# Seven-product FFN groups: two PSUM tiles in place of one, a list of weight jobs, and a last chunk of 512

## The chip, the cores and the metric

One Trainium2 chip, one of its cores. The metric is the device time of one launch in microseconds (us). The matrix engine is PE (its weight loads are PEld), the vector engine DVE, the scalar engine ACT; POOL and SP here issue transfers. SBUF is the on-chip memory, PSUM the accumulator of PE, in banks of 512 float32 per partition.

## The reference

A DiT block on 2048 tokens of width 1024: positions, modulated norm, a hybrid mixer (state-space branch and convolution branch), a second modulated norm, a SwiGLU FFN, and a final norm, in float32. The change touches the FFN of the second 1024 tokens and what follows it:

```
def _swiglu(h, wg, wu, wd):
    return (jax.nn.silu(h @ wg) * (h @ wu)) @ wd
...
x = x + g2 * _swiglu(_modulate(x, norm2_g[l], sh2, sc2), w_ffn_gate[l], w_ffn_up[l], w_ffn_down[l])
return _rmsnorm(x, norm_f_g)
```

The hidden width FFN_HIDDEN is 2816, that is 22 tiles of 128.

## The kernel before, in words

Every float32 product is made of three passes on PE: an operand is split into a rounded part hi (made by ACT) and a rest lo (made by DVE as a subtraction), and hi·hi, hi·lo and lo·hi are accumulated in PSUM. A matmul here is 128x128 weights by 512 tokens.

For the second half of the tokens the gate and up products of one hidden tile are a *group* of seven products in place of eight (a Strassen-like scheme over two halves of the tokens, L and R, and the weight matrices): products B11, T1, T2, B21, T3, B22, T4, named after their token operands, 12 matmuls each, 84 in all. They accumulate in three PSUM banks: b1 takes B11, then T2, T3 and T4 on top; b2 takes T1 and then B22; b3 takes B21. Between products the partial sums are read: ACT copies b1 after B11 (`fg`, left half), b2 after T1 (`fu`, right half), b1 after T2 (`fg`, right half); DVE adds b3 after B21, b1 after T3 (`fu`), b2 after B22 (`fg`); ACT applies silu; DVE multiplies `fu` by `fg` (right half, L1369) and, after T4, b1 by `fg` (left half, L1372); the result is split into ah and al. So the next product on b1 or b2 must come behind the read. In the kernel before, b1 and b2 are the two halves of one tile of two banks:

```
        ps, b3 = self.mm(), self.ms()
        b1, b2 = ps[:, 0:512], ps[:, 512:1024]
```

`mm()` gives one of three such tiles, `ms()` one of two tiles of one bank. The framework orders instructions by the tiles that they use, schedules them by priority, and puts in the semaphores.

Eleven chunks of two hidden tiles each follow one another. A chunk is two groups and a *down* part: 8 output tiles, each 12 matmuls with ah/al as moving operand and the weights `wd`; ACT scales the result out of PSUM (`fd`, L1424) and POOL adds it to the array d_x1 in device memory by an accumulating transfer (L1425). Chunk 0 computes its two tiles in the plain way, and its down part runs while DVE and ACT still make T1 to T4 in the background. The last chunk's down part adds into SBUF (L1440), first for the left 512 tokens (b=0), then for the right ones (b=1), with squares and their sum for the final norm; `final` then transposes, scales and stores the tokens.

The weights of a group (`group_weights`) are one load of 512 KB (wu, L1322) and two of 256 KB (gate, L1325 and L1326), four DVE sums (L1327 to L1331) in three buffers `ws`, and four conversions to hi (L1309) and lo (L1311) in two buffers each; the down weights are two loads with a conversion each (L1389, L1391). All are written at high priority and the scheduler places them. SP issues the loads in order; a load waits until its buffer's last reader is done. `t4()` is a ring of four buffers shared by fg, fu, fd and the background sums.

Of the kernel before, what the change touches and what calls it, by code (L numbers as in the profile page):

```python
# [22 lines left out]
HALF = 1024  # L23
# [20 lines left out]
class Kernel:  # L44
# [1243 lines left out]
    def prod(self, ps, w, c0, x, start=True, stop=True, group=True):  # L1288
# [4 lines left out]
        for k in range(n):  # L1293
            for j, (wt, mv) in enumerate(((whi, xhi), (whi, xlo), (wlo, xhi))):
                nc.tensor.matmul(  # L1295
                    ps,
                    wt[:, k, c0 : c0 + 128],
                    mv[k],
                    start=start and k == 0 and j == 0,
                    stop=stop and k == n - 1 and j == 2,  # L1300
                    skip_group_check=not group,
                )
            self.tick()

    def parts(self, f, c=1024):

        nc = self.nc
        hi = self.wp.tile([128, c // 128, 128], F32R, tag="hi", name=self.nm("hi"))
        nc.scalar.activation(hi, f, AF.Copy)  # L1309
        lo = self.wp.tile([128, c // 128, 128], F32R, tag="lo", name=self.nm("lo"))  # L1310
        nc.vector.tensor_tensor(lo, f, hi.bitcast(F32), op=OP.subtract)  # L1311
        return hi, lo

    def group_weights(self, vp, t):
# [5 lines left out]
        with self.tc.high_priority():  # L1320
            w4 = self.wp.tile([128, 8, 128], F32, tag="raw", name=self.nm("wu"))
            nc.sync.dma_start(w4, up)  # L1322
            w1, w2, w3 = (vp.tile([128, HALF], F32, tag="acc", name=self.nm("ws"), bufs=3).rearrange("p (k c) -> p k c", c=128) for _ in range(3))
            a, b = slice(0, 4), slice(4, 8)
            nc.sync.dma_start(w1[:, a], gate[:, a])  # L1325
            nc.sync.dma_start(w2[:, b], gate[:, b])  # L1326
            TT(w1[:, b], w4[:, a], w4[:, b], op=OP.add)  # L1327
            TT(w2[:, a], w1[:, b], w1[:, a], op=OP.subtract)
            p1 = self.parts(w1)
            TT(w3[:, a], w1[:, a], w4[:, a], op=OP.subtract)  # L1330
            TT(w3[:, b], w2[:, b], w2[:, a], op=OP.subtract)  # L1331
            p2 = self.parts(w2)
            p3 = self.parts(w3)
            p4 = self.parts(w4[:, b], 512)
        cut = lambda p, s: tuple(t[:, s] for t in p)
# [451 lines left out]
```

## Time and profile before

| | us |
|---|---|
| median of 3 runs | 3075.66 (3075.57, 3075.66, 3083.16) |
| the profiled execution | 3084.87, its span 3083.1 |
| PE busy | 2945.7 (96%) |
| DVE busy | 2089.6 (68%) |
| ACT busy | 1075.6 (35%) |

The profiled execution lies 9.21 us above the median of the runs; the 1.77 us between its time and its span lie outside the records. PE counts as busy from the start of a matmul to its modelled end, and matmuls overlap, so 96% still holds short stops. The second half's FFN lies from about 2345 us to the end of the span.

### The profile page before, as it was taken

How to read it: one execution, taken by the hardware profiler on the slowest of the kernel's cores; microseconds unless marked ns; L12 is line 12 of the kernel's file. 1: busy time of each engine (PE TensorE's matmuls, PEld its weight loads, DVE VectorE, ACT ScalarE, POOL GpSimd, SP SyncE). 2: the span in 40 equal slices, each digit the busy share in tenths (PEclk: the TensorE clock that was granted, in tenths of full speed). 3: DMA queues.
4: the chain of work that ended last, by engine and by line, in shares of the span. 5: the costliest groups of instructions: out<-in, count | busy, mean ns of one | idle time of the engine just before them, and what ended most of it. 6: DMA issues, size and time to landing. Idle time of an engine off the chain costs nothing.

```text
span 3083.1 us, 34510 instructions
## 1 busy us (share of the span) xinstructions
PE 2945.7 (96%) x12987; PEld 2357.3 (76%) x12987; DVE 2089.6 (68%) x3116; ACT 1075.6 (35%) x1463; POOL 245.3 (8%) x401
## 2 busy tenths in 40 slices
PE   7999999999999989999999999999998999999998
PEld 3778787878878768878888888888787677777776
DVE  6389899997887675668778787757567343333336
ACT  4223344333442662232212112233245333333333
POOL 0112321100011000000000000000000000011100
PEclk9999999999999999999999999999999999999999
DMA  5344545633443558764122212224566444445543
GB/s 199 123 122 129 152 161 172 184 97 115 125 119 116 185 191 293 259 204 151 62 62 76 62 62 62 89 97 148 177 207 144 102 103 103 103 107 118 121 106 130
DMA packets 391367, 411.29 MB, mean 133 GB/s; under 512 B 33377, under 2 KB 322497, under 8 KB 391200
## 3 DMA queue, kind: packets, MB, share of 16 engines
q1 hardware_dynamic: 339104, 275.73, 28.9%
q0 software_dynamic: 38640, 128.61, 15.4%
q10 hardware_dynamic: 13456, 4.75, 0.6%
q8 instruction: 102, 1.67, 0.2%
q14 instruction: 65, 0.53, 0.1%
HBM read 279.37 MB, written 129.61 MB: 133 GB/s over the span
## 4 chain that ended last, share of the span: by engine, by line
issue 51%; PE 32%; DVE 7%; DMA 5%; POOL 2%; ACT 2%; ACTq 0%; POOLq 0%; DVEq 0%; SPq 0%
PE mm L182 16%; PE mm L1295 11%; DVE acc L920 2%; DMA wm<-in_w_mod_dram 1%; PE ms L1295 1%; PE ms L741 1%; POOL d_x L1425 1%; DMA d_xt<-xts 1%; DVE lo L162 1%; DMA d_x<-fd 1%; PE ms L696 1%; POOL d_x L1112 1%; DMA Braw<-in_ssm_b_im_dram 0%; DMA dwr<-in_dw_kernel_dram 0%; PE mm L312 0%
## 5 line engine op out<-in xcount | busy, mean ns | idle before, releaser
L920 DVE SCALAR_TENSOR_TENSOR acc<-cin,dwk,acc 128x1009 f32<-128x1009 f32 (+1 forms) x464 | 570.6, 1272 | 1.1 <-ACT acc L916 0.5
L160 ACT ACTIVATE hi<-raw 128x1024 fp32r<-128x1024 f32 (+1 forms) x212 | 222.7, 1050 | 770.1 <-PE mm L182 726.5
L182 PE MATMUL mm<-hh,hi 128*128 128x512 f32 x1152 | 479.5, 416 | 0.5 <-ACT hh L446 0.5
L182 PE MATMUL mm<-hl,hi 128*128 128x512 f32 x1152 | 455.0, 395 | 0.0
L182 PE MATMUL mm<-hh,lo 128*128 128x512 f32 x1152 | 454.4, 394 | 0.0
L162 DVE TENSOR_TENSOR lo<-raw,hi 128x1024 fp32r<-128x1024 f32 (+1 forms) x212 | 256.5, 1210 | 93.4 <-ACT hi L160 93.0
L182 PE MATMUL mm<-h2h,hi 128*128 128x512 f32 x704 | 274.8, 391 | 0.0
L182 PE MATMUL mm<-h2l,hi 128*128 128x512 f32 x704 | 273.9, 389 | 0.1
L182 PE MATMUL mm<-h2h,lo 128*128 128x512 f32 x704 | 273.9, 389 | 0.0
L182 PEld LDWEIGHTS mm<-hh,lo 128*128 128x128 f32 x1152 | 218.2, 189 | 47.2 <-issue 0.4
L182 PEld LDWEIGHTS mm<-hh,hi 128*128 128x128 f32 x1152 | 218.4, 190 | 46.6 <-issue 2.2
L182 PEld LDWEIGHTS mm<-hl,hi 128*128 128x128 f32 x1152 | 218.7, 190 | 44.8 <-issue 1.6
L1311 DVE TENSOR_TENSOR lo<-ws,hi 128x1024 fp32r<-128x1024 f32 x60 | 73.5, 1225 | 230.6 <-ACT hi L1309 229.6
L182 PEld LDWEIGHTS mm<-h2l,hi 128*128 128x128 f32 x704 | 132.2, 188 | 27.9 <-DVE h2l L1145 0.5
L182 PEld LDWEIGHTS mm<-h2h,hi 128*128 128x128 f32 x704 | 132.2, 188 | 27.6 <-issue 0.3
L182 PEld LDWEIGHTS mm<-h2h,lo 128*128 128x128 f32 x704 | 132.2, 188 | 27.5
L1295 PE MATMUL mm<-al,hi 128*128 128x512 f32 x352 | 138.1, 392 | 4.9 <-DVE al L195 4.9
L1295 PE MATMUL mm<-ah,hi 128*128 128x512 f32 x352 | 135.0, 394 | 2.8 <-DVE fg L1406 2.4
L1295 PE MATMUL mm<-ah,lo 128*128 128x512 f32 x352 | 137.1, 389 | 0.0
L182 PE MATMUL mm<-ah,hi 128*128 128x512 f32 x352 | 136.7, 391 | 0.0
L182 PE MATMUL mm<-al,hi 128*128 128x512 f32 x352 | 136.7, 390 | 0.0
L182 PE MATMUL mm<-ah,lo 128*128 128x512 f32 x352 | 136.5, 389 | 0.0
(491 smaller groups left out, 5705.1 us busy)
## 6 DMA issues: line engine op xcount, KB each, us to landing
d_x<-fd POOLq DMA_DIRECT2D x80, 512.0 KB, 8.2
raw<-in_w_in_dram SPq DMA_DIRECT2D x72, 512.0 KB
wm<-in_w_mod_dram SPq DMA_DIRECT2D x48, 512.0 KB
d_g<-gsig POOLq DMA_DIRECT2D x32, 512.0 KB, 4.2
raw<-in_w_out_dram SPq DMA_DIRECT2D x32, 512.0 KB
raw<-in_w_ffn_gate_dram SPq DMA_DIRECT2D x28, 512.0 KB
raw<-in_w_ffn_up_dram SPq DMA_DIRECT2D x28, 512.0 KB
wd<-in_w_ffn_down_dram SPq DMA_DIRECT2D x24, 512.0 KB
```

The costliest lines, as they stand in the source:

```text
L160: nc.scalar.activation(hi, raw, AF.Copy)
L162: nc.vector.tensor_tensor(lo, raw, hi.bitcast(F32), op=OP.subtract)
L182: nc.tensor.matmul(ps[:, b * bw : (b + 1) * bw], wt[:, k, c0 : c0 + 128], mv[k][:, b * bw : (b + 1) * bw], start=(k == 0 and j == 0), stop ...
L696: nc.tensor.matmul(pz[:, d, :], BD[:, d, i, r, :], CR[d][r][:, i, d : d + 8].rearrange("p j c -> p (j c)"), start=(r == 0), stop=(r == 1))
L741: nc.tensor.matmul(ps.rearrange("p (i m) -> p m i", i=8), IN[:, d, i, :], rhs, start=True, stop=True)
L920: self.behind(nc.vector.scalar_tensor_tensor(t, x[:, i : i + W], K(i), t, op0=OP.mult, op1=OP.add), LAG)
L1112: nc.gpsimd.dma_start(self.d_x1[m, :, ts], xt)
L1295: nc.tensor.matmul(ps, wt[:, k, c0 : c0 + 128], mv[k], start=start and k == 0 and j == 0, stop=stop and k == n - 1 and j == 2, skip_group_ ...
L1311: nc.vector.tensor_tensor(lo, f, hi.bitcast(F32), op=OP.subtract)
L1425: nc.gpsimd.dma_start(self.d_x1[m4 * 4 + m, :, hs], o, accum_op=OP.add)
```

## The change

- b1 and b2 are tiles of their own, each the first half of a two-bank tile.
- The weights of groups and down parts are one list of *jobs* (four for a group, two for a down part). A job has a load, sums and a conversion. `next_job` is called at fixed places (after T1, B21, B22 and T4 are written, and after each half of a down part): it converts the job three ahead, sums the one five ahead and loads the one seven ahead. hi and lo have a third buffer. Conversions are ordered behind the last read of PSUM written before them. The down weights come through the same two buffers `raw` as the groups' up weights.
- The down part works on two output tiles at a time; in the first pair the hidden tile that was finished last comes at the end (`late`): its hi passes, then its lo pass.
- Nine chunks of two tiles, and the last four tiles (groups 18 to 21) as one chunk of 512 hidden units, whose down part is 192 matmuls into SBUF (96 for each half of the tokens). So 72 results go to d_x1 instead of 80; the number of matmuls is the same. `final` for the left half of the tokens starts, as it did, when the left half of the last down part is written; the right half behind it now has 96 matmuls instead of 48.

The core of the diff:

```diff
+    def stage(self, j, what):
+        nc = self.nc
+        if what == "load":
+            j["f"] = j["load"]()
+        elif what == "sums":
+            if j["sums"]:
+                j["sums"]()
+        else:
+            f = j["f"]() if callable(j["f"]) else j["f"]
+            n = self.ringed % 3
+            self.ringed += 1
+            out = []
+            for p in range(2):
+                if n < 2:
+                    t = self.wp.tile([128, 8, 128], F32R, tag=("hi", "lo")[p], name=self.nm("hl"[p]))
+                else:
+                    t = j["ring"][p]
+                c = 1
+                for x in j["shape"]:
+                    c *= x
+                out.append(t.rearrange("p k c -> p (k c)")[:, 0:c].rearrange("p (k c) -> p k c", k=j["shape"][0]))
+            hi, lo = out
+            i = nc.scalar.activation(hi, f, AF.Copy)
+            if self.last_act:
+                self.order(i, self.last_act)
+            i = nc.vector.tensor_tensor(lo, f, hi.bitcast(F32), op=OP.subtract)
+            if self.last_dve:
+                self.order(i, self.last_dve)
+            j["w"] = (hi, lo)
+
+    def jobs_start(self):
+        self.done = -1
+        self.last_act = self.last_dve = None
+        for n in range(7):
+            self.stage(self.jobs[n], "load")
+        for n in range(5):
+            self.stage(self.jobs[n], "sums")
+        for n in range(3):
+            self.stage(self.jobs[n], "conv")
+
+    def next_job(self):
+
+        self.done += 1
+        for what, n in (("conv", 3), ("sums", 5), ("load", 7)):
+            if self.done + n < len(self.jobs):
+                self.stage(self.jobs[self.done + n], what)
...
+        def sums1():
+            TT(w[1][:, b], w[4][:, a], w[4][:, b], op=OP.add)
+
+        def sums2():
+            TT(w[2][:, a], w[1][:, b], w[1][:, a], op=OP.subtract)
+
+        def sums3():
+            TT(w[3][:, a], w[1][:, a], w[4][:, a], op=OP.subtract)
+            TT(w[3][:, b], w[2][:, b], w[2][:, a], op=OP.subtract)
+
+        r = ring["w"]
+        return [
+            self.job((8, 128), r, load1, sums1),
+            self.job((8, 128), r, load2, sums2),
+            self.job((8, 128), r, load3, sums3),
+            self.job((4, 128), r, lambda: w[4][:, b]),
+        ]
...
-        ps, b3 = self.mm(), self.ms()
-        b1, b2 = ps[:, 0:512], ps[:, 512:1024]
+    def group(self, J, X, a):
+        b1, b2, b3 = self.mm()[:, 0:512], self.mm()[:, 0:512], self.ms()
...
+        self.prod(b1, W(2, 0), 0, X["T3"], start=False, group=False)
         with hp():
             add(u[:, R], b1)
+        self.prod(b2, W(2, 1), 0, X["B22"], start=False, group=False)
         with hp():
             add(g[:, R], b2)
+            act(g[:, R], g[:, R], AF.Silu)
             nc.vector.tensor_tensor(u[:, R], u[:, R], g[:, R], op=OP.mult)
+        self.next_job()
+        self.prod(b1, J[3]["w"], 0, X["T4"], start=False, group=False)
         with hp():
             nc.vector.tensor_tensor(u[:, L], b1, g[:, L], op=OP.mult)
+            act(a[0], u)
+            self.last_dve = nc.vector.tensor_tensor(a[1], u, a[0].bitcast(F32), op=OP.subtract)
+        self.next_job()
...
+    def down_prods(self, to, w, late):
+
+        for ps, x, c in to if not late else ():
+            self.prod(ps, w, c, x)
+        if late:
+            n = len(to[0][1][0]) - 1
+            first, last = slice(0, n), slice(n, n + 1)
+            for s, passes in ((first, (0, 1, 2)), (last, (0, 2)), (last, (1,))):
+                for ps, x, c in to:
+                    self.prod(ps, [t[:, s] for t in w], c, [p[s] for p in x], start=s is first, group=False, passes=passes)
...
+        acc = lambda dt: vp.tile([128, HALF], dt, tag="acc", name=self.nm("wx"), bufs=3)
+        ring = {"n": 0, "w": [acc(F32R).rearrange("p (k c) -> p k c", c=128) for _ in range(2)]}
+        ring["f"] = [acc(F32), vp.tile([128, HALF], F32, tag="csum", name="wx")]
+        ring["f"] += [vp.tile([128, HALF + 30], F32, tag="cin", name=self.nm("wx"), bufs=2)[:, 0:1024] for _ in range(2)]
+        self.jobs, self.ringed = [], 0
+        downs, groups = {}, {}
+        for c in range(9):
+            if c:
+                for t in (2 * c, 2 * c + 1):
+                    groups[t] = self.group_jobs(ring, t)
+            downs[c] = self.down_jobs(ring, 2 * c, 2)
+        for t in range(18, 22):
+            groups[t] = self.group_jobs(ring, t)
+        downs[9] = self.down_jobs(ring, 18, 4) + self.down_jobs(ring, 18, 4)
+        self.jobs_start()
+        for c in range(9):
             if c:
                 for t in range(2):
-                    self.group(vp, c * 2 + t, X, *a[t])
+                    self.group(groups[2 * c + t], X, a[t])
                     yield "up"
-            if c == 10:
-                break
-            for m4 in range(2):
-                w = down(c, m4)
-                for m in range(4):
-                    ps = self.mm()
-                    for b in range(2):
-                        self.prod(ps[:, b * 512 : (b + 1) * 512], w, m * 128, halves[b])
-                    o = self.t4(name="fd")
-                    nc.scalar.activation(o, ps, AF.Copy, scale=self.mod2[:, 24 + m4 * 4 + m : 25 + m4 * 4 + m])
-                    nc.gpsimd.dma_start(self.d_x1[m4 * 4 + m, :, hs], o, accum_op=OP.add)
-                    yield "down"
+            for i, J in enumerate(downs[c]):
+                for m in range(0, 4, 2):
+                    pp = [self.mm(), self.mm()]
+                    to = [(ps[:, b * 512 : (b + 1) * 512], half(b), (m + n) * 128) for n, ps in enumerate(pp) for b in range(2)]
+                    self.down_prods(to, J["w"], i == 0 and m == 0)
+                    for n, ps in enumerate(pp):
+                        o = self.t4(name="fd")
+                        r = i * 4 + m + n
+                        nc.scalar.activation(o, ps, AF.Copy, scale=self.mod2[:, 24 + r : 25 + r])
+                        nc.gpsimd.dma_start(self.d_x1[r, :, hs], o, accum_op=OP.add)
+                self.next_job()
+                yield "down"
+        for t in range(2):
+            self.group(groups[18 + t], X, a[t])
+            yield "up"
+        a = a + [(self.slot("P", name="ah"), self.slot("P", name="al")) for _ in range(2)]
+        for t in range(2):
+            self.group(groups[20 + t], X, a[2 + t])
+            yield "up"
...
+                J = downs[9][b * 4 + m // 2]
+                if m % 2 == 0:
+                    pp = [self.mm()[:, bs] for _ in range(2)]
+                    self.down_prods([(ps, half(b), n * 128) for n, ps in enumerate(pp)], J["w"], b == 0 and m == 0)
+                    self.next_job()
+                ps = pp[m % 2]
...
-        take(f1, 2 + 8)
+        take(f1, 2 + 2)
         self.finish(e)
-        take(f1, 10 * 2 + 9 * 8 + 8)
+        take(f1, 8 * 2 + 8 * 2 + 4 + 8)
         acc = end[0]
```

Three places show what stands where now. The first is PE in a group of a middle chunk, before; mm is the tile with b1 and b2, ms is b3, and the second name is the weight part:

```order
L1295 MATMUL mm_20718<-T2h_16967,lo_20708 128x512
L1295 MATMUL ms_20719<-B21h_16651,lo_20708 128x512
L1295 MATMUL mm_20718<-T3h_16970,hi_20710 128x512 [waits Activation_49]
...
L1295 MATMUL mm_20718<-T3h_16971,lo_20712 128x512
L1295 MATMUL mm_20718<-B22h_16654,hi_20710 128x512 [waits DVE_49]
...
L1295 MATMUL mm_20718<-B22h_16655,lo_20712 128x512
L1295 MATMUL mm_20718<-T4h_17473,hi_20714 128x512 [waits DVE_49]
```

The same place in the changed kernel (b1 is mm_18075, b2 is mm_18076):

```order
L1296 MATMUL mm_18075<-T2h_16967,wx_17358 128x512
L1296 MATMUL ms_18077<-B21h_16650,wx_17357 128x512
...
L1296 MATMUL ms_18077<-B21h_16651,wx_17358 128x512
L1296 MATMUL mm_18075<-T3h_16970,h_18068 128x512 [waits Activation_49]
...
L1296 MATMUL mm_18075<-T3h_16971,l_18069 128x512
L1296 MATMUL mm_18076<-B22h_16654,h_18068 128x512
...
L1296 MATMUL mm_18076<-B22h_16655,l_18069 128x512
L1296 MATMUL mm_18075<-T4h_17457,h_18106 128x512 [waits DVE_49]
```

Before, one matmul of B21 is left between T2 and T3, and T3, B22 and T4 each begin with a wait. Now all of B21 stands between T2 and T3, and B22 carries no wait of its own; T3 and T4 still wait for the reads of b1.

The second place is DVE from the read of b3 to the split of the second group of a chunk, before (lo<-wd are the lo parts of the down weights, lo<-wu that of the up weights):

```order
L1347 TENSOR_TENSOR fg_20847<-ms_20846,fg_20847 128x512 [waits DMASW4_49,DMASW0_49,PE_49]
L1311 TENSOR_TENSOR lo_20843<-wu_20818,hi_20841 128x512 [waits Activation_49]
L1347 TENSOR_TENSOR fu_20848<-mm_20845,fu_20848 128x512 [waits DMASW5_49,DMASW1_49,PE_49]
L1347 TENSOR_TENSOR fg_20847<-mm_20845,fg_20847 128x512 [waits PE_49,Activation_49]
L1391 TENSOR_TENSOR lo_20949<-wd_20945,hi_20947 128x1024 [waits DMAHW6_49,Activation_49]
L1369 TENSOR_TENSOR fu_20848<-fu_20848,fg_20847 128x512 [waits Activation_49]
L1372 TENSOR_TENSOR fu_20848<-mm_20845,fg_20847 128x512 [waits PE_49]
L1391 TENSOR_TENSOR lo_21019<-wd_21015,hi_21017 128x1024 [waits DMAHW7_49,Activation_49]
L195 TENSOR_TENSOR al_16977<-fu_20848,ah_16976 128x1024 [waits Activation_49]
```

And now (L1337 makes a lo part, L1390 to L1396 are weight sums for the next chunk's first group, L1456 and L1460 the two products, L1462 the split):

```order
L1432 TENSOR_TENSOR fg_18078<-ms_18077,fg_18078 128x512 [waits DMASW4_49,DMASW0_49,PE_49]
L1337 TENSOR_TENSOR wx_17358<-wd_18019,wx_17357 128x1024 [waits DMAHW1_49,Activation_49]
L1432 TENSOR_TENSOR fu_18079<-mm_18075,fu_18079 128x512 [waits DMASW5_49,DMASW1_49,PE_49]
L1432 TENSOR_TENSOR fg_18078<-mm_18076,fg_18078 128x512 [waits PE_49]
L1456 TENSOR_TENSOR fu_18079<-fu_18079,fg_18078 128x512 [waits Activation_49]
L1390 TENSOR_TENSOR wx_17359<-wu_18072 128x512 [waits DMAHW5_49]
L1337 TENSOR_TENSOR l_18170<-wd_18051,h_18169 128x1024 [waits DMAHW4_49,Activation_49]
L1460 TENSOR_TENSOR fu_18079<-mm_18075,fg_18078 128x512 [waits PE_49]
L1393 TENSOR_TENSOR wx<-wx_17359 128x512 [waits DMAHW0_49,DVE_49]
L1396 TENSOR_TENSOR wx_17361<-wx_17359,wu_18072 128x512
L1462 TENSOR_TENSOR al_16977<-fu_18079,ah_16976 128x1024 [waits Activation_49]
```

The lo part of the first down weights has moved up, ahead of the read of b1 after T3, and a weight sum that needs a load of `wu` (L1390) stands now between the two products; two more sums stand ahead of the split.

The third place is PE at the start of the next down part in the changed kernel (ah_16974 is the first hidden tile, 16976 and 16977 the second; the tiles mm_18198 and mm_18199 are the first pair, and the latter reuses the buffer of the group's b1):

```order
L1296 MATMUL mm_18075<-T4h_17458,l_18107 128x512
L1296 MATMUL mm_18198<-ah_16974,wx_17357 128x512 [waits Activation_49]
...
L1296 MATMUL mm_18199<-ah_16974,wx_17357 128x512 [waits DVE_49]
...
L1296 MATMUL mm_18230<-ah_16974,wx_17357 128x512 [waits DVE_49]
L1296 MATMUL mm_18198<-ah_16976,wx_17357 128x512 [waits Activation_49]
...
L1296 MATMUL mm_18198<-al_16977,wx_17357 128x512 [waits DVE_49]
...
L1296 MATMUL mm_18230<-al_16975,wx_17357 128x512
```

Six matmuls of the first hidden tile stand ahead of the first that needs the group's b1 to be free, and the lo pass of the second hidden tile is now last.

## Rows read from the trace of the kernel before

**Rows 1.** The page, part 1: busy us, share of the span, instructions.
```profile
PE 2945.7 (96%) x12987; PEld 2357.3 (76%) x12987; DVE 2089.6 (68%) x3116; ACT 1075.6 (35%) x1463; POOL 245.3 (8%) x401
```

**Rows 2.** Waits of PE from 2340 to 3075 us: us in total, times, longest.
```profile
PE mm L1295 <- DVE fg L1347: 17.5, 20, 1.2
PE mm L1295 <- DVE fu L1347: 15.7, 20, 0.8
PE mm L1295 <- ACT fg L1346: 15.0, 21, 0.8
PE mm L1295 <- DVE al L195: 4.9, 10, 0.5
```

**Rows 3.** Windows: one chunk, and its second group; busy by engine, PEclk, DMA share.
```profile
2855.00:2922.90 67.90, 62.63 (x265) 48.63 (x264) 25.27 (x30) 25.84 (x31) 6.81 (x8) 1.00 0.49 109
...
2877.60:2900.20 22.60, 20.21 (x85) 15.37 (x84) 10.67 (x13) 7.50 (x10) 0.00 (x0) 1.00 0.17 49
```

**Rows 4.** Timeline of PE in the first group: start, length, instruction, [idle before <-releaser].
```profile
2864.55 0.39 PE L1295 MATMUL mm<-T2h,hi 128*128 128x512 f32 x1
...
2865.91 0.39 PE L1295 MATMUL ms<-B21h,lo 128*128 128x512 f32 x1
2867.05 0.50 PE L1295 MATMUL mm<-T3h,hi 128*128 128x512 f32 x1 [0.75 <-ACT fg L1346]
...
2869.67 0.39 PE L1295 MATMUL mm<-T3h,lo 128*128 128x512 f32 x1
2870.85 0.50 PE L1295 MATMUL mm<-B22h,hi 128*128 128x512 f32 x1 [0.78 <-DVE fu L1347]
...
2873.49 0.39 PE L1295 MATMUL mm<-B22h,lo 128*128 128x512 f32 x1
2874.74 0.50 PE L1295 MATMUL mm<-T4h,hi 128*128 128x512 f32 x1 [0.85 <-DVE fg L1347]
```

**Rows 5.** Timeline of DVE in the second group: the read of b2, then a lo part.
```profile
2896.60 0.69 DVE L1347 TENSOR_TENSOR fg<-mm,fg 128x512 f32<-128x512 f32 x1 [3.22 <-PE mm L1295]
2897.44 1.23 DVE L1391 TENSOR_TENSOR lo<-wd,hi 128x1024 fp32r<-128x1024 f32 x1
```

**Rows 6.** Timeline of ACT there: silu, and the split's hi part.
```profile
2897.33 0.63 ACT L1368 ACTIVATE fg<-fg 128x512 f32<-128x512 f32 x1
...
2901.19 1.04 ACT L194 ACTIVATE ah<-fu 128x1024 fp32r<-128x1024 f32 x1
```

**Rows 7.** A load in a quiet stretch: its issue on SP, and two windows behind it.
```profile
2867.65 0.37 SPq L1322 DMA_DIRECT2D wu<-in_w_ffn_up_dram  x1
```
```profile
2870.50:2871.00 0.50, 0.15 (x1) 0.16 (x2) 0.29 (x1) 0.00 (x0) 0.00 (x0) 1.00 0.40 116
2871.00:2871.50 0.50, 0.50 (x3) 0.41 (x4) 0.00 (x0) 0.00 (x0) 0.00 (x0) 1.00 0.00 0
```

**Rows 8.** A load under a down part: its issue on SP, and the DVE sum behind it.
```profile
2846.45 0.37 SPq L1325 DMA_DIRECT2D ws<-in_w_ffn_gate_dram  x1
```
```profile
2858.58 0.69 DVE L1328 TENSOR_TENSOR ws<-ws 128x512 f32<-128x512 f32 x1 [1.27 <-DMA ws<-in_w_ffn_gate_dram]
```

**Rows 9.** The first group: PE's timeline, and a window of it (PEclk 0.69).
```profile
2373.06 0.50 PE L1295 MATMUL mm<-B11h,hi 128*128 128x512 f32 x1 [2.69 <-ACT fd L1424]
...
2380.62 0.51 PE L1295 MATMUL ms<-B21h,lo 128*128 128x512 f32 x1 [2.04 <-DVE lo L1311]
```
```profile
2374.00:2385.00 11.00, 8.75 (x24) 6.05 (x23) 7.16 (x11) 4.81 (x6) 1.84 (x3) 0.69 0.94 164
```

**Rows 10.** The end: timelines of PE and DVE, and the window behind the last down matmul.
```profile
3058.95 2.79 PE L1493 MATMUL mm<-ident,x 128*128 128x128 f32 x24
3061.58 0.95 PE L962 MATMUL ms<-onesm,rsf 128*128 128x1 f32 x8
```
```profile
3070.16 0.15 DVE L141 TENSOR_SCALAR nv<-ms 128x4 f32<-128x4 f32 x1
...
3078.63 0.74 DVE L1482 TENSOR_SCALAR o<-ms,ny 128x512 f32<-128x512 f32 x1
```
```profile
3058.70:3083.10 24.40, 15.33 (x106) 14.59 (x104) 16.84 (x72) 7.95 (x14) 2.13 (x4) 0.81 0.49 194
```

More of the change, by code (lines that the diff above doesn't have):

```diff
@@ L1286, in sums_last, with prod @@
             yield 2.8
-    def prod(self, ps, w, c0, x, start=True, stop=True, group=True):
+    def prod(self, ps, w, c0, x, start=True, stop=True, group=True, passes=(0, 1, 2)):
         nc = self.nc
@@ L1298, in prod @@
                     mv[k],
-                    start=start and k == 0 and j == 0,
-                    stop=stop and k == n - 1 and j == 2,
+                    start=start and k == 0 and j == passes[0],
+                    stop=stop and k == n - 1 and j == passes[-1],
                     skip_group_check=not group,
@@ L1319, in group_weights @@
         gate, up = (self.A[n][0, :, col].rearrange("(k p) c -> p k c", p=128) for n in ("w_ffn_gate", "w_ffn_up"))
[L1320 to L1334, printed above, removed]
@@ L1335, in group_weights, with take, load1 @@
-        cut = lambda p, s: tuple(t[:, s] for t in p)
-        return {"A11": cut(p1, a), "S1": cut(p1, b), "S2": cut(p2, a), "A12": cut(p2, b), "S3": cut(p3, a), "S4": cut(p3, b), "A22": p4}
-    def group(self, vp, t, X, ah, al):
+        w = {}
+        a, b = slice(0, 4), slice(4, 8)
+        def take():
+            i = ring["n"] % 4
+            ring["n"] += 1
+            return ring["f"][i].rearrange("p (k c) -> p k c", c=128)
+        def load1():
+            w[4] = self.wp.tile([128, 8, 128], F32, tag="raw", name=self.nm("wu"))
+            nc.sync.dma_start(w[4], up)
+            w[1] = take()
+            nc.sync.dma_start(w[1][:, a], gate[:, a])
+            return w[1]
@@ new lines, in load2, with load3 @@
+        def load2():
+            w[2] = take()
+            nc.sync.dma_start(w[2][:, b], gate[:, b])
+            return w[2]
+        def load3():
+            w[3] = take()
+            return w[3]
+        def sums1():
[5 more added lines that the diff above has]
+            TT(w[3][:, b], w[2][:, b], w[2][:, a], op=OP.subtract)
@@ new lines, in group_jobs, with down_jobs, load @@
+        r = ring["w"]
[5 more added lines that the diff above has]
+        ]
+    def down_jobs(self, ring, c0, cn):
+        n = 1024 // cn
+        def load(i):
+            raw = self.wp.tile([128, cn, n], F32, tag="raw", name=self.nm("wd"))
+            self.nc.sync.dma_start(raw, self.A["w_ffn_down"][0, c0 * 128 : (c0 + cn) * 128, i * n : (i + 1) * n].rearrange("(k p) c -> p k c", p=128))
+            return raw
+        return [self.job((cn, n), ring["w"], lambda i=i: load(i)) for i in range(cn)]
@@ L1356, in group @@
+        self.next_job()
+        self.prod(b1, W(1, 0), 0, X["T2"], start=False, group=False)
         with hp():
-            copy(g[:, R], b1)
-        self.prod(b3, W["A12"], 0, X["B21"])
+            act(g[:, R], b1)
+        self.prod(b3, W(1, 1), 0, X["B21"])
         with hp():
             add(g[:, L], b3)
-            nc.scalar.activation(g[:, L], g[:, L], AF.Silu)
-        self.prod(b1, W["S3"], 0, X["T3"], start=False, group=False)
+            act(g[:, L], g[:, L], AF.Silu)
+        self.next_job()
@@ L1380, in ffn_s @@
         a = X["a"]
[L1381 to L1393 removed]
+        half = lambda b: [[t[p][:, b * 512 : (b + 1) * 512] for t in a] for p in range(2)]
         for b in range(2):
```

54 lines of the change are left out of this document (18 added, 36 removed).

## The prediction

> **What bounds the kernel now.** I read the page first: PE is busy 96% of the span, and no other engine comes near [rows 1]. So only two things can move the time much: fewer matmuls, which this change does not bring, or fewer stops between them. The waits of PE in the second FFN say where the stops are: 20 groups, and in each one wait for the DVE read `fg`, one for the DVE read `fu` and one for the ACT copy `fg`, 17.5 + 15.7 + 15.0 us in all; `al` adds 4.9 us at ten starts of a down part [rows 2]. The timeline shows how long such a stop is for PE itself. Unhindered, matmuls start every 0.227 us (six steps in 1.36 us). From the last matmul of B21 to the first of T3 there are 1.14 us, from T3 to B22 1.18, from B22 to T4 1.25, so 0.91 + 0.95 + 1.02 = 2.89 us are lost in the three [rows 4]. Against the windows: a group of 84 matmuls takes 22.60 us [rows 3], while 84 x 0.2267 = 19.04; 3.56 us are lost, the three stops and 0.67 us of slower pitch right behind each restart. The rest of the chunk, 67.90 - 2 x 22.60 = 22.70 us [rows 3], is the down part with 96 x 0.2267 = 21.76, so 0.94 us are lost there.
>
> The stop at B22 is a false one: B22 goes to b2, but waits for the read of b1, because the two are one tile. The stops at T3 and T4 are true ones, but as long as they are only because nothing stands between the product before and the next one on the same bank: a read begins 0.50 us behind the last matmul (the `fg` add that released T4 is 0.69 us long and ended just ahead of 2874.74; the last B22 started at 2873.49 [rows 4, 5]).
>
> **The groups.** With b1 and b2 apart and B21 whole behind T2, each read of a bank has a product of 12 matmuls, 2.72 us, as cover. T3 needs the copy after T2: 0.5 us and then about 0.6 (ACT's other pass over 128x512, silu, takes 0.63 [rows 6]), inside B21. B22 needs the copy after T1, long done. T4 needs the `fu` add after T3. Here DVE's order counts, since in the second group of a chunk the lo part of the first down weights now stands ahead of that add. I put the start of the `fg` add after B22 at zero. T4 could start at -0.27. B21 ended at -5.95, its add runs -5.45 to -4.76, silu (0.63 [rows 6]) to -4.1, the hi part (about 1.04, as the other ACT pass over 128x1024 [rows 6]) to -3.0, the lo part (1.23 [rows 5]) to -1.8, the `fu` add to -1.1. That is 0.8 us ahead of T4. So no stop is left in a group: 19 x 3.56 = 67.6 us (the first group is taken apart below). If the cover failed at T4 alone, 1 us per group would come back.
>
> **The PSUM buffers.** What the rows say first: before, no wait stands at B11 or T1, whose tile is fresh in every group [rows 2]. Now a group takes two of the three tiles, so T1 of a chunk's second group reuses the b1 of the first one, which DVE reads last, with the left product. That product comes behind the right product (from +1.4) and a lo part (from about 2.45, when its hi part is done, to 3.6), and ends at +4.3; T1 wants the bank at +5.2. I count nothing, with 0.9 us to spare; if DVE were 1.5 us later, 11 such places would cost 0.6 each, 7 us. The Trainium skill, "Perfetto Trace Analysis", section Matmul Optimizations, asks that all eight PSUM banks be used; this change leaves half of two tiles idle in every group, and by that rule T1's wait would be the one to appear and the time about 3005. No row here can show it, since before there is no such reuse.
>
> **The start of a down part.** Before, 0.94 us lost, ten times, 9.4 us. Now there are eight such starts behind groups. On DVE a pass over 128x512 takes 0.69 and one over 128x1024 1.23 [rows 5]; I let each overlap the next by 0.08. The order is right product (+1.4 to 2.0), the sum L1390 (to 2.6), the lo part of the second down weights (to 3.8), left product (to 4.5). PE ends T4 at +2.45, has six matmuls (to 3.8), and then needs the left product's bank: a stop of 0.75 us. Behind it ah (1.04 [rows 6]) is there at 5.6, wanted at 6.1; al, behind two more sums, at 6.8, wanted at 7.9. So 8 x 0.75 = 6.0 us, a gain of 3.4. The start of the last down part has more matmuls of finished tiles ahead of it; I count no stop.
>
> The sum L1390 needs the load of `wu`, which SP can issue only when the lo part of the first down weights has read its buffer, at -1.8. A quiet load of this size, issued at 2867.65, moved its last bytes ahead of 2871.0 [rows 7], 3.35 us. So it lands at about +1.7, and DVE wants it at +2.0. The bound from above is a load that shared the stretch with the accumulating transfers: issued at 2846.45, its reader started at 2858.58, 12.1 us [rows 8]. I take the quiet one: the second group of a chunk lies over 22 us behind the down part, and its DMA share is 0.17 [rows 3].
>
> **The first group.** It lost 2.69 us at its start to results on their way out and 2.04 us to a lo part, and over 11 us the granted clock was 0.69, which on 8.75 busy us is 2.7 us more [rows 9]: 7.4 us, and the 3.56 of every group. The new order has the weights converted earlier, but the results still wait for the same transfers. Bounds 0 and 11; I take 4.5, which leaves one stop of the kind and some of the low clock.
>
> **The end.** Behind the last down matmul 24.40 us pass [rows 10]. With 96 matmuls in place of 48 in the right half (taken from elsewhere, so neutral), the comparison is 21.8 + 24.4 = 46.2 us. Now the 32 transposes of `final` (2.79 us for 24 [rows 10], so 3.7) go among the matmuls. Behind the last one are left: 2.6 us until the one-column products, 0.95 of these, a Newton step whose first instruction had waited until 3070.16 behind `final`'s own work (twelve small steps like that first one of 0.15 [rows 10], 1.8 us without and an estimated 2.3 with the time between them), three scalings of 0.74, and 4.5 us from the last scaling to the end (3078.63 to 3083.1 [rows 10]): about 13. That is 38.5 us plus what PE waits for DVE among the transposes, between 0 and 12; I take 6, as three of the four sets stand right behind a DVE chain. Gain 1.7, bounds +7.7 and -4.3.
>
> **The sum.** 67.6 + 3.4 + 4.5 + 1.7 = 77.2 us. Against the profiled execution, 3084.87 - 77.2 = 3007.7. It lies 9.2 us above the median of the runs; the same difference from 3075.66 gives **2998**. Accumulating transfers, 72 in place of 80, and the other loads lie beside PE's work and count nothing.
>
> **The rivals.**
> *DVE blocked on the new sum's load.* If each load took the 12.1 us of [rows 8], it would land at +10.3, 8.3 us too late, and everything behind it on DVE, the left product first, with it: 8 x 8.3 = 66 us, 3065. A mild form, 5.5 us, costs 8 x 1.9 = 15: 3013. Against it: the quiet stretch. For it: only 0.3 us to spare. The Trainium skill, "Trainium Kernel Development and Optimization", section Key Constraints, says that transfers of all queues run on the same 16 DMA engines and interleave; here that would stretch this load with any transfer beside it, towards the 3065. Rows 7 and 8 agree with it, 3.35 against 12.1 us.
> *The same, on the other side.* The kernel becomes slower when that load takes longer than 3.7 + 77.2 / 8 = 13.4 us in every chunk; at 16 us, queued behind two gate loads as well, 8 x 12.3 = 98 us are lost and the time is 3097.
> *A read of PSUM stays late.* If ACT's hi parts run a microsecond or two later than in my chain, the `fu` add misses T4 by about 1 us in each group (or B22 waits after all, 0.95): 19 to 20 us, 3017.
> *The end or T1 on the bad side* gives 3004 to 3005, within my range.
>
> **How the numbers follow.** Forecast 0.70, with a range of its own of 2985 to 3012 (first group, end and T1 at their bounds, not all together). Late read 0.11; mild load 0.10; load of 12 us 0.05; slower 0.04. For 8 in 10 the range takes in both the late read and the mild load: 2984 to 3019. A difference of 0.3%, 9 us, is about what a measurement of this kernel can tell from none. Faster: 0.70 + 0.11 + 0.10 and more than half of the 0.05, 0.94; same 0.02; slower 0.04.
>
> **What would show it.** A group of 19.0 to 19.3 us in the windows, no wait of PE at T3, B22, T4 or T1; a stop of 0.5 to 1 us behind six matmuls of each down part, released by the left product; DVE at L1390 not waiting for a DMA for more than some tenths. Wrong would be a DVE wait for `wu` of several us, groups above 20 us, or an end that lasts over 50 us from the right half's first matmul.

## The result, and the profile after

The changed kernel takes 2990.86 us (median of 4 runs, 2987.68 to 2991.67); the kernel before, with the runs made beside it, 3079.41. The ratio is 0.9706, with a 95% interval from 0.968 to 0.9732: 2.9% faster. Forecast were 2998 us and a range of 2984 to 3019.

The profiled execution took 2991.20 us, its span is 2989.4. Page, part 1:

```profile
PE 2911.4 (97%) x12987; PEld 2357.1 (79%) x12987; DVE 2087.4 (70%) x3118; ACT 1066.0 (36%) x1457; POOL 238.4 (8%) x393
```

The same number of matmuls, 34 us less of PE's busy time (a matmul behind a restart counts as longer), and 94 us less span. What answers to [rows 2], the waits of PE from 2340 to 2990 us:

```profile
PE mm L1296 <- ACT fg L1430: 1.7, 1, 1.7
PE mm L1296 <- DVE fu L1432: 1.2, 1, 1.2
PE mm L1296 <- ACT fd L1526: 1.0, 1, 1.0
PE mm L1296 <- DVE o L1610: 0.5, 1, 0.5
```

Before, four rows with 20, 20, 21 and 10 waits; now one wait each, 4.4 us together. What answers to [rows 3], the windows of one chunk, of its second group, of its down part, and then of the right half of the last down part and of the tail behind it (busy of PE, PEld, DVE, ACT, POOL, then PEclk, DMA share, GB/s):

```profile
2787.73:2847.81 60.08, 60.08 (x265) 49.48 (x264) 24.84 (x30) 25.57 (x31) 6.52 (x8) 1.00 0.56 123
2806.77:2825.81 19.04, 19.04 (x85) 15.77 (x84) 9.04 (x11) 7.37 (x10) 0.00 (x0) 1.00 0.22 70
2825.81:2847.81 22.00, 22.00 (x97) 17.94 (x96) 9.80 (x13) 10.69 (x11) 5.67 (x7) 1.00 0.78 147
2947.96:2974.42 26.46, 25.99 (x129) 21.49 (x129) 23.51 (x76) 10.62 (x17) 1.60 (x3) 1.00 0.15 60
2974.42:2989.40 14.98, 8.51 (x73) 8.13 (x71) 7.27 (x19) 3.05 (x5) 0.53 (x1) 0.92 0.45 176
```

A group takes 19.04 us, which is 84 matmuls at 0.2267 and nothing else; a chunk takes 60.08, where 264 matmuls take 59.85. The timeline of PE in that second group, against [rows 4]:

```profile
2817.43 0.39 PE L1296 MATMUL ms<-B21h,wx 128*128 128x512 f32 x1
2817.65 0.39 PE L1296 MATMUL mm<-T3h,h 128*128 128x512 f32 x1
...
2820.14 0.39 PE L1296 MATMUL mm<-T3h,l 128*128 128x512 f32 x1
2820.37 0.39 PE L1296 MATMUL mm<-B22h,h 128*128 128x512 f32 x1
...
2822.86 0.39 PE L1296 MATMUL mm<-B22h,l 128*128 128x512 f32 x1
2823.09 0.39 PE L1296 MATMUL mm<-T4h,h 128*128 128x512 f32 x1
```

From product to product 0.22 to 0.23 us, where there were 1.14, 1.18 and 1.25.

The second FFN starts with the same matmul in both, and this is where the account has to start too, since the program ahead of it is the same:

```profile
2341.59 0.39 PE L1296 MATMUL mm<-ah,h 128*128 128x512 f32 x1
```

Before, that matmul stood at 2344.97. So 3.4 of the 93.7 us between the two spans come from the unchanged part, and the FFN itself went from 738.1 to 647.8 us: 90.3 us saved. By stretches: from its start to the second group 56.1 to 44.6 (11.5 saved); the other 19 groups and the down parts between them 634.9 to 539.3, of which 21.8 us are the 96 matmuls that moved to the end (73.8 saved); from the last group's T4 to the end 47.1 to 63.9, with those 96 matmuls (5.0 saved).

### The profile page after: what moved, and what is told of

Read it like the earlier page. It is cut to its first block, busy times and chain, and to the rows that moved or that the text cites. A ratio compares the mean times of both kernels' runs of the same rounds, so it can differ in the third digit from the quotient of the medians.

```text
span 2989.4 us, 34432 instructions
## 1 busy us (share of the span) xinstructions
PE 2911.4 (97%) x12987; PEld 2357.1 (79%) x12987; DVE 2087.4 (70%) x3118; ACT 1066.0 (36%) x1457; POOL 238.4 (8%) x393
## 4 chain that ended last, share of the span: by engine, by line
issue 46%; PE 39%; DVE 6%; DMA 5%; POOL 2%; ACT 1%; ACTq 0%; POOLq 0%; DVEq 0%; SPq 0%
PE mm L1296 18%; PE mm L182 16%; DVE acc L920 2%; PE ms L1296 2%; DMA wm<-in_w_mod_dram 1%; PE ms L741 1%; DVE lo L162 1%; DMA d_xt<-xts 1%; DMA d_in<-st 1%; POOL d_x L1112 1%; PE ms L696 0%; DMA ma<-d_ma 0%; PE mm L312 0%; DMA Braw<-in_ssm_b_re_dram 0%; DMA dwr<-in_dw_kernel_dram 0%
## 5 line engine op out<-in xcount | busy, mean ns | idle before, releaser
L182 PEld LDWEIGHTS mm<-h2l,hi 128*128 128x128 f32 x704 | 132.2, 188 | 28.1 <-DVE h2l L1145 0.5
L182 PE MATMUL mm<-al,hi 128*128 128x512 f32 x352 | 136.8, 390 | 0.0
L182 PE MATMUL mm<-ah,hi 128*128 128x512 f32 x352 | 136.7, 391 | 0.0
L182 PE MATMUL mm<-ah,lo 128*128 128x512 f32 x352 | 136.6, 389 | 0.0
L182 PE MATMUL mm<-mgh,hi 128*128 128x512 f32 x256 | 101.7, 398 | 4.5 <-DVE xt L1111 3.3
L1337 DVE TENSOR_TENSOR l<-wx,h 128x1024 fp32r<-128x1024 f32 x40 | 48.9, 1223 | 81.0 <-ACT h L1334 81.0
L182 PE MATMUL mm<-vbh,hi 128*128 128x512 f32 x256 | 101.2, 395 | 0.9 <-DVE o L1610 0.9
L182 PE MATMUL mm<-mgl,hi 128*128 128x512 f32 x256 | 100.8, 394 | 0.9 <-DVE mgl L195 0.9
```

What stands on the lines that cost most here:

```text
L182: nc.tensor.matmul(ps[:, b * bw : (b + 1) * bw], wt[:, k, c0 : c0 + 128], mv[k][:, b * bw : (b + 1) * bw], start=(k == 0 and j == 0), stop ...
L1337: i = nc.vector.tensor_tensor(lo, f, hi.bitcast(F32), op=OP.subtract)
```

## The experiments

Each ran on one chip beside the kernel before. Stretches of the profiles are compared where the effect is smaller than what executions differ by ahead of the FFN.

**The two tiles alone**, on the kernel before:

```diff
-        ps, b3 = self.mm(), self.ms()
-        b1, b2 = ps[:, 0:512], ps[:, 512:1024]
+        b1, b2, b3 = self.mm()[:, 0:512], self.mm()[:, 0:512], self.ms()
```

> The kernel before, with b1 and b2 as two tiles and nothing else of the change. Theory A, the shared tile alone made the stops: with the read of each bank covered by another product a group falls from 22.6 to about 19.2 us, 19 groups save about 65 us, and the time is 2.1% below the kernel before (ratio 0.979, some 3012). Theory B, the list of jobs with its third buffer is needed for it: with two buffers stops come back at B11, T2 or T4, released by hi or lo parts of weights, a group takes 20 to 21.5 us, and only 20 to 50 us are saved (ratio 0.984 to 0.994).

Ratio 0.975 (0.9731 to 0.9769), 3006.04 us. Windows of its second group of a chunk and of the down part behind it:

```profile
2571.16:2590.20 19.04, 19.04 (x85) 15.77 (x84) 11.19 (x15) 7.72 (x10) 0.00 (x0) 1.00 0.19 55
2590.20:2612.93 22.73, 22.25 (x97) 17.87 (x96) 5.18 (x6) 10.81 (x11) 5.98 (x7) 1.00 0.81 166
```

The groups are already at 19.04 us, the down part is still as long as before. Theory A holds, two weight buffers suffice, and the gain is a little larger than expected: the 19 groups with the down parts save 68.5 us (634.9 to 566.4), and the first stretch saves 7.3 (56.1 to 48.8), which the expectation had not counted. In that stretch the first group alone went from 28.0 to 21.0 us.

**One tile again**, on the changed kernel (the reverse of the edit above).

> The changed kernel, with b1 and b2 again as the halves of one tile. Theory A: B22 and T4 stop again for the read of the other half, 0.95 and about 0.95 us in each of 19 groups, 36 us, some 3027. Theory B, the look-ahead of the jobs lets PE fill such stops: the order of instructions puts 4 or 5 matmuls of the next group or of B21 ahead of each stop (0.9 to 1.1 us against reads of 1.2), so 0.2 to 0.7 us per group are left, 4 to 13 us, 2995 to 3004.

Ratio 0.9829 (0.9815 to 0.9844), 3032.24 us: 41 more than the changed kernel; the FFN alone takes 685.2 us against 647.8, 37.4 more. The size is A's (36), the place is not. PE's timeline in one chunk, at B22 and T4 of its first group and at the start of its down part:

```profile
2582.00 0.50 PE L1296 MATMUL mm<-B11h,l 128*128 128x512 f32 x1 [0.39 <-DVE l L1337]
...
2582.81 0.40 PE L1296 MATMUL mm<-B22h,h 128*128 128x512 f32 x1
...
2586.48 0.50 PE L1296 MATMUL mm<-T4h,wx 128*128 128x512 f32 x1
...
2610.95 0.50 PE L1296 MATMUL mm<-ah,h 128*128 128x512 f32 x1 [0.79 <-DVE fu L1461]
```

PE does fill the holes with the next group's B11, as theory B said. But in the second group it fills them with matmuls of the down part, and these then lack at its start, where PE waits for the left product. This chunk takes 63.50 us, 3.4 more than in the changed kernel: PE is idle for 1.4 of them, and for the rest its matmuls start further apart (it is busy for 62.07 us, where 60.08 do). So with the rest of the change but one tile a chunk keeps 3.7 of the 8.1 us that it lost before: the rest gives back about half, and does not replace the second tile.

**No late order** in the down parts:

```diff
-                    self.down_prods(to, J["w"], i == 0 and m == 0)
+                    self.down_prods(to, J["w"], False)
```

> The changed kernel, with no pair of a down part in the late order. Theory A, this order took the stop of 0.94 us away from the starts of down parts and 2.4 us from chunk 0: nine matmuls stand ahead of the first that needs ah of the second tile and twelve ahead of al, which came 4.3 us behind T4 in the changed kernel; a stop of about 1.6 us in each of 8 chunks and one of about 2.4 in chunk 0, together 15 us, some 3006. Theory B, the places came free by the other order of the conversions: less than 0.3 us each, 2991 to 2994.

Ratio 0.9742 (0.9728 to 0.9757), 3005.77 us. A chunk takes 61.56 us, 1.48 more, as theory A says. PE's timeline at the start of its down part:

```profile
2717.73 0.39 PE L1296 MATMUL mm<-ah,h 128*128 128x512 f32 x1
...
2719.68 0.50 PE L1296 MATMUL mm<-ah,h 128*128 128x512 f32 x1 [0.44 <-DVE fu L1460]
...
2722.04 0.50 PE L1296 MATMUL mm<-al,h 128*128 128x512 f32 x1 [0.29 <-DVE al L1462]
```

For chunk 0 theory A fell: its down part takes 23.3 us here and 23.5 in the changed kernel, so the 2.4 us that were won there are not the late order's. With the two tiles alone it is 27.8, so another part of the change won them; the section on the prediction shows what stood in the way.

**A last chunk of 256** in place of 512 (ten chunks in the loop, groups 20 and 21 and a down part of 96 matmuls behind it):

```diff
-        for c in range(9):
+        for c in range(10):
...
-        for t in range(18, 22):
+        for t in range(20, 22):
...
-        downs[9] = self.down_jobs(ring, 18, 4) + self.down_jobs(ring, 18, 4)
+        downs[10] = self.down_jobs(ring, 20, 2) + self.down_jobs(ring, 20, 2)
```

> The changed kernel, with ten chunks of two tiles and a last one of two tiles (256) in place of nine and one of four. Theory A, the long right half of the last down part covers the scaling and storing of the left half: with 48 matmuls in it instead of 96 the vector engine's chain sticks out again, 4 to 6 us at the end, and one more start of a down part, some 2995 to 2997. Theory B, the end is the same chain of the last result in both: within 1.5 us of the changed kernel.

Ratio 0.9726 (0.9709 to 0.9742), 3000.24 us. The window from the last T4 to the end:

```profile
2951.83:2999.10 47.27, 36.79 (x202) 30.89 (x200) 36.95 (x104) 14.85 (x23) 2.14 (x4) 0.92 0.29 112
```

47.3 us, where the kernel before has 47.1; in the changed kernel it is 63.9 less 21.8, so 42.1, and by its second profile (64.8, the next run) 43.0. Theory A: 5.2 or 4.3 us. The FFN as a whole takes 651.6 us, 3.8 or 2.7 more than in the two profiles of the changed kernel (647.8 and 648.95). That is less than at the end, since no group of this run has the one stop at T4 that is taken apart below. (The larger difference in the medians lies ahead of the FFN: its first matmul stands at 2347.52 in this profile.)

**Four on one chip.** First the changed kernel itself, to set the others beside it.

> The changed kernel itself, unchanged, to set beside the three others of this call on the same chip. Ratio to the kernel before 0.9706 again, within 0.002.

Ratio 0.9717 (0.9704 to 0.973), 2997.78 us. Its FFN takes 648.95 us against 647.8 in the first profile, though the span is 7.6 us longer.

**The left half stored last:**

```diff
-        e = self.bg(self.final(1, acc, 0, 4))
         take(f1)
+        e = self.bg(self.final(1, acc, 0, 4))
```

> The changed kernel, with the scaling and storing of the left half of the tokens begun only when the right half of the last down part is written, instead of among its matmuls. Theory A, the 5 us that the end gained in the changed kernel come from this overlap: the 32 transposes and the four chains of the vector engine go back behind the last down matmul, the stretch from the last group to the end grows from 63.9 to 67 to 69 us, 3 to 5 us slower. Theory B, the transposes only take PE's time wherever they stand and the tail is the chain of the last result: within 1.5 us of the changed kernel.

Ratio 0.9725 (0.9709 to 0.9741), 3003.02 us. Windows from the last T4 to the end, of the right half, and of the tail:

```profile
2933.55:3001.20 67.65, 58.94 (x298) 50.25 (x296) 42.48 (x108) 19.56 (x28) 2.14 (x4) 0.92 0.31 109
2955.56:2977.50 21.94, 21.94 (x98) 18.08 (x98) 13.88 (x24) 6.18 (x9) 0.00 (x0) 1.00 0.00 1
2977.50:3001.20 23.70, 14.99 (x105) 14.21 (x103) 15.71 (x70) 7.52 (x13) 2.14 (x4) 0.78 0.52 200
```

The stretch is 67.65 us, against 64.79 in the changed kernel on this chip: 2.9 us, just below what theory A gave, and above theory B. The overlap costs the right half 4.5 us (26.47 against 21.94) and takes 8.7 from the tail (14.99 against 23.70); in the left half the changed kernel was 1.3 us longer here, with two short waits for ah. Against the first profile of the changed kernel (63.9) it is 3.7 us. The medians' interval could not have told this; the stretch does, though the changed kernel's own two profiles differ by 0.9 us in it.

**The weight sum behind the read of PSUM:**

```diff
+            i = TT(w[1][:, b], w[4][:, a], w[4][:, b], op=OP.add)
+            if self.last_read:
+                self.order(i, self.last_read)
```

> The changed kernel, with the first weight sum of a group ordered behind the last read of PSUM by the vector engine that is written ahead of it. In the order of instructions the sum L1390 then stands behind the left product in the first group of the last chunk, instead of ahead of the read of b3. Theory A, the one stop of 1.33 us at T4 there came from this sum, which waited 5.3 us for its load with the reads of PSUM queued behind it: the stop goes, 1 to 1.5 us faster, all else alike. Theory B, the read was late by the lo parts alone: no change.

In the changed kernel one group of the twenty stops at T4. In its first profile, DVE there, the issue of the load it waits for, and PE:

```profile
2860.65 0.69 DVE L1390 TENSOR_TENSOR wx<-wu 128x512 f32<-128x512 f32 x1 [5.31 <-DMA wu<-in_w_ffn_up_dram]
2861.26 0.68 DVE L1432 TENSOR_TENSOR fg<-ms,fg 128x512 f32<-128x512 f32 x1
```
```profile
2855.37 0.37 SPq L1375 DMA_DIRECT2D wu<-in_w_ffn_up_dram  x1
```
```profile
2865.47 0.50 PE L1296 MATMUL mm<-T4h,h 128*128 128x512 f32 x1 [1.18 <-DVE fu L1432]
```

With the sum moved, that group takes 19.04 us (2853.79 to 2872.83), where it took 20.25 in the changed kernel on the same chip. Theory A: 1.2 us in that stretch. In the medians it does not show, 2996.42 and a ratio of 0.9713 (0.9699 to 0.9727).

**That, and earlier transposes:**

```diff
+            if b:
+                self.rate = 2.0
```

> As the one before, and the background work is given credit at a rate of 2.0 in the right half of the last down part, so that the transposes of the left half come earlier among its matmuls. If the tail of 15.0 us is held up by the fourth of these chains (its last scaling on the vector engine ended 0.1 us ahead of the add of the last result, which then began 1.2 us late), 1 to 1.5 us more are saved, 2 to 3 us in all; if the earlier chains make PE wait for their reads instead, as much is lost in the right half.

2998.94 us, 0.9719 (0.9705 to 0.9734): nothing gained. The tail fell to 14.1 us, but the right half rose to 28.5; PE waited there for the background's values instead. The other side of the expectation.

**Idle additions ahead of the left product**, two and four:

```diff
             nc.vector.tensor_tensor(u[:, R], u[:, R], g[:, R], op=OP.mult)
+            for _ in range(2):
+                pad = nc.vector.tensor_tensor(g[:, R], u[:, R], g[:, R], op=OP.add)
...
+            i = nc.vector.tensor_tensor(u[:, L], b1, g[:, L], op=OP.mult)
+            self.order(i, pad)
```

> The changed kernel, with two idle additions of 128x512 on the vector engine between the right product and the left product of every group (they go into values that nothing reads any more; the result is the same). This makes the left product some 1.2 us later and asks how much cover is left at T1 of the next group, which reuses the tile that the left product reads, and at the start of a down part. By the times of the changed kernel the left product ended 1.1 us ahead of T1, and 0.8 us ahead of the matmul that reuses its tile in the down part; al ended 0.5 us ahead of its first matmul. Theory A (the tile of two banks makes T1 wait once this cover is used up): a stop of 0.1 to 0.3 us at T1 and 0.7 to 1.0 at each down part, a chunk goes from 60.1 to 61.0 to 61.4 us, 8 to 12 us in all. Theory B (other things hide it, and there is more cover than I see): a chunk below 60.3 us.

> The same with four additions, 2.4 us later. Theory A: a stop of 1.3 to 1.5 us at T1 of the second group, 2.0 to 2.3 at the down part, a chunk of 63.4 to 63.9 us, 28 to 34 us in all. Theory B: the scheduler's other orders and the background cover take part of it, a chunk below 62.5 us.

Ratios 0.9744 (0.9727 to 0.976) and 0.9836 (0.9815 to 0.9856). The second group and the down part of one chunk, with two additions and then with four:

```profile
2631.64:2650.68 19.04, 19.04 (x85) 15.77 (x84) 10.11 (x13) 7.37 (x10) 0.00 (x0) 1.00 0.24 69
2650.68:2673.43 22.75, 22.34 (x97) 17.86 (x96) 11.02 (x15) 10.25 (x10) 5.14 (x6) 1.00 0.70 132
```
```profile
2653.64:2672.68 19.04, 19.04 (x85) 15.77 (x84) 11.31 (x15) 7.37 (x10) 0.00 (x0) 1.00 0.22 69
2672.68:2699.46 26.78, 23.97 (x97) 19.00 (x96) 12.21 (x17) 10.54 (x10) 5.14 (x6) 0.94 0.60 114
```

At T1 theory A fell: no stop, not even with four additions, and both groups of the chunk stay at 19.04 us. At the down part it held with two, and there all of the chunk's loss lies: 0.75 us more with two, 4.8 with four, more than twice what A gave. The chunks are 60.83 and 64.86 us. With four, other weight sums slipped in between the additions, so the left product came 3.6 us later, not 2.4. The first row shows which matmul waits, the second what followed:

```profile
2678.25 0.50 PE L1296 MATMUL mm<-ah,wx 128*128 128x512 f32 x1 [2.69 <-DVE fu L1462]
```
```profile
2678.25:2684.00 5.75, 5.62 (x16) 4.17 (x17) 4.12 (x5) 2.62 (x3) 0.00 (x0) 0.70 0.16 47
```

It is the thirteenth of the down part: twelve ran from 2672.68 on. Behind this stop the granted clock fell: it is 0.70 in the second row, so for part of these 5.75 us PE ran at the lower of its two levels, 1.2 GHz. PE is busy for 23.97 us in this down part and for 22.00 in the changed kernel's, so of the 4.8 us 2.8 are standing still and 2.0 slower work. And T1 of the second group began before the left product had even started to read the first group's b1, here PE and then DVE:

```profile
2656.36 0.39 PE L1296 MATMUL mm<-T1h,h 128*128 128x512 f32 x1
```
```profile
2657.04 0.68 DVE L1462 TENSOR_TENSOR fu<-mm,fg 128x512 f32<-128x512 f32 x1
```

## Why the prediction was right, and where it was off

**The groups (67.6 us forecast).** Right in place, size and cause. With the tiles alone 19 groups and the unchanged down parts save 68.5 us. Every read of a bank has a product as cover, and no other part of the change is needed for it; the rest of the change without the second tile recovers about half of a chunk's loss.

**The start of a down part (3.4 forecast, about 6.7 measured).** This step was mis-sized, and its error has a name: the prediction took the second tile of the pair to reuse the buffer of the group's b1, and so a stop of 0.75 us behind six matmuls. The trace of the changed kernel, DVE first and then PE:

```profile
2825.29 0.68 DVE L1390 TENSOR_TENSOR wx<-wu 128x512 f32<-128x512 f32 x1
2825.89 1.22 DVE L1337 TENSOR_TENSOR l<-wd,h 128x1024 fp32r<-128x1024 f32 x1
2827.03 0.68 DVE L1460 TENSOR_TENSOR fu<-mm,fg 128x512 f32<-128x512 f32 x1
```
```profile
2825.81 0.39 PE L1296 MATMUL mm<-ah,wx 128*128 128x512 f32 x1
...
2826.95 0.62 PE L1296 MATMUL mm<-ah,wx 128*128 128x512 f32 x2
2827.40 0.39 PE L1296 MATMUL mm<-al,wx 128*128 128x512 f32 x1
```

DVE is where the prediction had it, the left product ends 1.9 us behind T4 (2.05 forecast). But the seventh matmul starts at 2827.17 (the second of the two in one row) while that product still reads until 2827.71: another buffer. The additions show that the third tile, behind twelve matmuls, is the one, 2.7 us of cover and not 1.4. So 0.94 us at each of nine starts became 0.2 at each of eight, 8.5 to 1.8 (60.08 less 59.85, eight times); the tenth start of before lies in the end's stretch. The 68.5 of the groups, plus 6.7, less the one stop of 1.33 us that is told next, make the 73.8 of the middle stretch to 0.1. The order of instructions shows that a matmul waits for DVE, not for which of its operations; the sentence ahead of the prediction that says which buffer is reused is wrong in the same way. What the late order is worth is the run without it: 1.5 us for each chunk.

**The sum's load.** Forecast: landed at +1.7, wanted at +2.0. It was issued at 2821.44 and its sum started without a wait at 2825.29, so it took at most 3.85 us. The rival of a blocked DVE happened twice, in the first two groups of the last chunk, where no down weights stand between two loads of `wu`. DVE waited 5.3 us in the first, which cost PE a stop of 1.33 us that went with the order of that sum, and 3.6 us in the second, which cost PE nothing:

```profile
2879.42 0.69 DVE L1390 TENSOR_TENSOR wx<-wu 128x512 f32<-128x512 f32 x1 [3.59 <-DMA wu<-in_w_ffn_up_dram]
```

The first of these loads was waited for till 2860.65, 5.3 us behind its issue; the last accumulating transfer had been issued at 2850.14, and these take a median of 8.5 us in the middle chunks of the changed kernel. The second was issued at 2875.85 and took 3.6 us, near the 3.35 that the forecast took for a quiet load. The windows of the load that was in time and of the first of these two:

```profile
2821.44:2825.29 3.85, 3.85 (x19) 3.19 (x18) 1.88 (x4) 1.27 (x2) 0.00 (x0) 1.00 0.48 140
2855.37:2860.65 5.28, 5.28 (x25) 4.38 (x24) 0.00 (x0) 0.60 (x1) 0.00 (x0) 1.00 0.72 175
```

At 140 GB/s the first window moved 0.54 MB, little more than the load itself (512 KB, 0.52 MB); the second moved 0.92 MB, so 0.40 MB of other transfers ran beside its load. This is the mild form of the rival, with a stop in one place of twenty. The 12.1 us that the prediction took as the bound from above were read from a gate load of 256 KB, half the size of this one, so they are no bound for a load of `wu`; what the changed kernel shows for one is at most these 5.3 us. The rule of the Trainium skill, "Trainium Kernel Development and Optimization", section Key Constraints, is that transfers issued from the SP, ACT and POOL queues all run on the same 16 DMA engines and interleave; this trace agrees with it, 5.3 us beside other transfers against 3.6 to 3.85 with next to none.

**The PSUM buffers.** Nothing was counted for T1, and nothing came; but the prediction's chain, by which T1 had 0.9 us to spare, is not the reason: with four additions T1 began 0.7 us ahead of the left product, so it does not get the buffer that this product reads. The rule of the Trainium skill, "Perfetto Trace Analysis", section Matmul Optimizations, is that all eight banks be used; as the prediction read it, T1 would have waited, and no run here shows that. In these runs the half-empty tiles cost nothing at T1, since the next one free was one that had been read early.

**The first group (4.5 forecast, 11.5 measured).** Mis-sized twice. First, the group itself: 7.0 of its 28.0 us went with the two tiles alone. The whole group before, with the tiles alone, and in the changed kernel:

```profile
2373.06:2401.08 28.02, 23.88 (x84) 17.46 (x85) 15.32 (x21) 10.15 (x14) 2.54 (x3) 0.88 0.47 91
2367.73:2388.71 20.98, 20.98 (x85) 16.94 (x86) 14.42 (x20) 10.05 (x14) 2.55 (x3) 0.92 0.62 118
2365.11:2386.17 21.06, 19.41 (x86) 15.69 (x85) 10.17 (x15) 8.95 (x12) 1.70 (x2) 1.00 0.69 143
```

PE stood still for 4.1 us before and not at all with the tiles alone; the other 2.9 are slower work, at a granted clock of 0.88 before and 0.92 then. In the changed kernel the clock is 1.00, but the group is no shorter, because a stop is back:

```profile
2372.39 0.50 PE L1296 MATMUL mm<-T2h,h 128*128 128x512 f32 x1 [1.65 <-ACT fg L1430]
```
```profile
2371.74 0.60 ACT L1430 ACTIVATE fg<-mm 128x512 f32<-128x512 f32 x1 [1.71 <-DMA d_x<-fd]
```

T2 waits for the copy of b1 after B11, and this copy had to wait 1.71 us for a buffer whose result was still on its way to d_x1. So the prediction was right that results still wait for these transfers, and wrong in how much that costs. Second, chunk 0's down part gave 4.6 us (28.1 to 23.5). The sum had only one of its stops, the 2.69 us at its end; PE's wait of 2.35 us for `fg` within it was left out. What stood in its way, in the kernel before, on DVE:

```profile
2344.02 0.69 DVE L1328 TENSOR_TENSOR ws<-ws 128x512 f32<-128x512 f32 x1 [0.34 <-DMA ws<-in_w_ffn_gate_dram]
...
2346.70 0.69 DVE L1331 TENSOR_TENSOR ws<-ws 128x512 f32<-128x512 f32 x1 [1.38 <-DMA ws<-in_w_ffn_gate_dram]
...
2350.83 0.68 DVE L1406 TENSOR_TENSOR fg<-mm,fg 128x512 f32<-128x512 f32 x1
```

The last gate product of chunk 0 (L1406) stood behind the sums of the next group's weights, which waited for their loads; PE waited 2.35 us for it. In the changed kernel it ran at 2341.79, ahead of the sums, and PE did not wait for it; of the waits for results on their way out 1.03 us are left. No run tests this order by itself. The row was there to be read before (a single wait for `fg` L1406 in the second FFN, 2.4 us), and the prediction passed over it.

**The end (1.7 forecast, 5.0 measured; 4.1 on the other chip).** The mechanism was right, its size was off: stops of PE among the transposes were put at 6 us and came out near 1 (26.46 us in which 96 matmuls take 21.8 and 32 transposes, at the forecast's price, 3.7), and the tail is 15.0 us where 13 were forecast. The last chunk of 512 is worth 4.3 to 5.2 us at the end, and 2.7 to 3.8 of the whole FFN, since it brings the one stop at T4; the overlap itself is worth 2.9 to 3.7.

Sum by these stretches: 73.8 + 11.5 + 5.0 = 90.3 us, against 77.2 forecast. That the forecast of 2998 misses the median by only 7 us is partly luck. From profile to profile it misses by 16.5 (3007.7 against 2991.20): 13.1 in the FFN and 3.4 in the unchanged part ahead. It was then lowered by the 9.2 us by which the profile of before lay above its median, and the profile of the changed kernel lies only 0.3 above its own. None of the runs is clearly better than the changed kernel; the moved sum saves 1.2 us in its stretch, which the medians can't show.

## What to carry to other kernels

Where a framework orders by tiles, as this one does, two accumulators in one tile wait for each other's readers; give each a tile of its own, and put one whole product between a bank's read and its next use. Look at each stop for what stands queued ahead of the released instruction on its engine, since a prefetched sum that waits for a load holds up everything behind it. Which buffer a pool hands out next can't be told by counting in turn: read it from the first matmul that starts while the old reader is still busy.

## What the runs showed of the hardware that was not expected

The same program, unchanged and with the same order of instructions, reached the first matmul of the second FFN at 2341.59 us in one profile and at 2348.05 in another, while the FFN behind it took 647.8 and 648.95. The two runs with idle additions, whose edits lie behind that matmul, reached it on one chip at 2340.96 and 2346.98. So executions differ by several us in the part ahead, for a reason that no run here shows, and hardly in the part where PE is the bound; effects of a few us are better read from stretches.
